# Up weights' second load cut in two, two products of the first step moved, and the last block's sums copied into PSUM before its last splits

## The chip, the core and the metric

The kernel runs on one core of one Trainium2 chip. The metric is the device time of one execution in microseconds. The core has a matrix engine (PE; its weight loads are shown as PEld), three engines for elementwise work (VectorE or DVE, ScalarE or ACT, GpSimd or POOL), SyncE (SP), which here only issues transfers, and 16 DMA engines that all queues share. Engines run side by side; each takes its own instructions in order and waits for the others by semaphores.

## The reference

Four layers on a residual stream of 512 tokens by 1024 features: attention with low-rank keys and values (MLA), an MLP, gated linear attention (GLA), an MLP, and a last RMS norm. All is float32. The change touches the two MLPs, cut to what matters:

```python
def sq_relu_mlp(xn, w_up, w_down):          # w_up 1024 x 4096, w_down 4096 x 1024
    hid = jnp.square(jax.nn.relu(xn @ w_up))
    return hid @ w_down

for i in range(DEPTH):                      # DEPTH = 2
    ...
    x = x + sq_relu_mlp(rms_norm(x, norm_mlp[i]), mlp_w_up[i], mlp_w_down[i])
return rms_norm(x, final_norm)
```

## The kernel before, in words

Every float32 operand of a matmul is split into a rounded high part and a rest (`split`: the high part by ACT, line 110, the rest by DVE, line 113), and each product is three matmuls: high by high, high by low, low by high. A weight tile is split into buffers named `wh` and `wl`, four of each, so that a split can run up to four products ahead of PE.

`mlp` works through the 4096 hidden columns in 8 blocks of 512 (`FB`, `NB`). In the first 7 blocks two multiplications with the weights are each done in 7 products instead of 8, by Strassen's scheme in Winograd's form: sums of quadrants of the weights and of the activations are multiplied, and the results added up in SBUF tiles `S11`, `S12`, `SU`, `S21`, `S5` (the first four lie in the memory of `xT`, and the profile names them so). A step of the loop makes 7 up products for the next block (24 matmuls of 128x256 each, line 958) and 7 down products for the present one (12 matmuls of 128x512 each, line 967). `step_in_halves` (steps 1 to 6) does all the up products and then all the down products. `step` (step 0 of each MLP) mixes them, in an order written as a tuple of functions: `up_t2`, `down_11` and so on. The up products are called "11", T1, T2, "21", T3, "22" and T4 here. In a step with halves they stand in the order 11, T1, T2, 21, T3, 22, T4.

The weights of a step come as named tiles. `fetch(b, name)` loads them for step `b`:

- `A1` and `A2`: 256 columns of the up weights each, 1 MB, in tiles `wraw` of which there are two. `A2`'s first half (`s3`, used by T3) must also have the block "A11" added to it; POOL does so with an accumulating transfer (line 937), which is a software transfer from its own queue. Its second half (`a22`) is used by T4.
- `S1`, `dS1`, `dS3`: 512 KB plain, to which POOL's queue accumulates another 512 KB (line 947). `d11`, `d12`, `d22`: 512 KB plain. All lie in `comb` tiles, one buffer for each name.

A tile is loaded for step `b + 1` when step `b` has split it for the last time: after each product the program calls `after(name)`, which calls `fetch(b + 1, name)`. SP issues the plain transfers in the order of these calls and waits in turn for each buffer to come free, so a load behind a waiting one waits too; POOL does the same with the accumulations, each of which waits until its plain part has landed. In the last step `after` calls `before_next` (first MLP) or `at_the_end` (second MLP), which load what follows.

Two more rules set the order. Instructions are put in order by a scheduler when the program is built, so ACT and DVE hold the splits of later products among the copies and squares of earlier ones. And in a step with halves, "11" goes into the PSUM bank `z`; ACT copies it to `y` (`copied`, line 1090) before T2 may add to `z`.

After the loop the second MLP makes the last block in the plain way, together with the last norm: the sums `S12` and `S11` are copied into PSUM banks (`two_banks("e")` and `("d")`, line 1258), products of the hidden tiles (split by `parts_of_quad`) are added to them there (`row`, line 1272), in the order of token tiles 2, 3, 0, 1, and then the same is done for the other half of the columns.

```python
            for product in (up_t2, down_11, up_t1, down_22, up_22, down_12, up_t3, down_5, down_21, up_t4):
                product()
        ...
            up_product(z, a11, "11", True)
            copied(y, z)
```

Of the kernel before, what the change touches and what calls it, by code (L numbers as in the profile page):

```python
# [18 lines left out]
P = 128  # L19
# [3 lines left out]
ND = D // P  # L23
# [27 lines left out]
def trunk_kernel(ctx: ExitStack, tc: tile.TileContext, t_in: dict, out: bass.AP):  # L51
# [27 lines left out]
    def two_banks(tag):  # L79
        return psum["pool"].tile([P, 1024], F32, tag=f"ps_{tag}", bufs=1, name=uname("ps2"))  # L80
# [302 lines left out]
    def col_chunk(w2d, c0, n):  # L383
        return load(w2d[:, c0 : c0 + n].rearrange("(k p) n -> p k n", p=P), w2d.shape[0] // P, n)
# [430 lines left out]
    def mlp(layer, nrm, nxt=None):  # L815
# [106 lines left out]
        def up_quadrant(b, c, h):  # L922
            cs = slice((b + 1) * FB + c * 256, (b + 1) * FB + c * 256 + 256)
            return w_up[h * KH * P : (h + 1) * KH * P, cs].rearrange("(k p) n -> p k n", p=P)
# [7 lines left out]
        def fetch(b, name):  # L932
            if name in ("A1", "A2"):
                c = int(name[1]) - 1
                W[name] = col_chunk(w_up, (b + 1) * FB + c * 256, 256)
                if c:
                    POOL.dma_start(W[name][:, :KH], up_quadrant(b, 0, 0), accum_op=ALU.add)
                return None
            q = up_quadrant if name == "S1" else down_quadrant
            W[name] = t = by_k(comb(home[name]), KH if name == "S1" else 2)  # L940
            plain, more = {
                "d11": ((0, 0), None), "d12": ((0, 1), None), "d22": ((1, 1), None),
                "S1": ((1, 1), (1, 0)), "dS1": ((1, 1), (1, 0)), "dS3": ((1, 0), (0, 0)),
            }[name]
            first_part = SP.dma_start(t, q(b, *plain))
            if more:
                POOL.dma_start(t, q(b, *more), accum_op=ALU.add)
            return first_part
# [21 lines left out]
        def step(b, q, r, after):  # L970
            opening = nxt is not None
            (q11, q12), (q21, q22) = q

            def begun(src):
                t = two_banks("e")
                ACT.activation(t, src, AF.Copy)
                return t

            def add(total, t):
                if opening:  # L980
                    ACT.activation(total, t, AF.Copy)
                else:
                    DVE.tensor_tensor(total, t, total, ALU.add)

            def onto(tag, total, a, parts, fresh=False):
                t = two_banks(tag)
                if not fresh:
                    ACT.activation(t, total, AF.Copy)
                down_product(t, a, parts, fresh)
                ACT.activation(total, t, AF.Copy)  # L990

            A1, A2, s1 = W["A1"], W["A2"], W["S1"]
            a11, a12, s3, a22 = A1[:, :KH], A1[:, KH:], A2[:, :KH], A2[:, KH:]
            d11, d12, ds1, ds3, d22 = (W[n] for n in ("d11", "d12", "dS1", "dS3", "d22"))

            z = bank("u")
            up_product(z, a11, "11", True)
            y = bank("u")
            ACT.activation(y, z, AF.Copy)

            d = two_banks("d")
            down_product(d, d11, parts_of_quad(q11), True)
            if opening:
                ACT.activation(S11, d, AF.Copy)
            e = two_banks("e") if opening else begun(d)

            up_product(y, a12, "21", False)
            finish(y, 0, 0, r)
            DVE.tensor_tensor(a11, s1, a11, ALU.add)

            down_product(e, d12, parts_of_quad(q21), opening)
            DVE.tensor_tensor(S11, e, S11, ALU.add)
            DVE.tensor_tensor(d11, ds1, d11, ALU.add)
            DVE.tensor_tensor(q12, q22, q12, ALU.subtract)
            DVE.tensor_tensor(q11, q11, q12, ALU.add)

            part = {"e": e}

            def down_11():
                down_product(d, d11, parts_of_quad(q11, -1.0), False)  # L1020
                part["e"] = begun(d)
                DVE.tensor_tensor(d12, d11, d12, ALU.add)
                after("d11")

            def up_t2():
                up_product(z, a11, "T2", False)
                u = part["u"] = tmp()
                ACT.activation(u, z, AF.Copy)
                DVE.tensor_tensor(a12, a11, a12, ALU.add)

            def up_t1():
                w = part["w"] = bank("u")
                up_product(w, s1, "T1", True)
                w2 = part["w2"] = bank("u")
                ACT.activation(w2, w, AF.Copy)
                after("S1")

            def down_22():
                e = part["e"]
                down_product(e, d12, parts_of_quad(q22), False)  # L1040
                add(S12, e)
                after("d12")

            def down_12():
                down_product(d, ds3, parts_of_quad(q12), False)
                add(SU, d)
                after("dS3")
                DVE.tensor_tensor(q22, q22, q11, ALU.subtract)

            def up_22():  # L1050
                w = part["w"]
                up_product(w, a12, "22", False)
                c = tmp()
                DVE.tensor_tensor(c, w, part["u"], ALU.add)
                finish(c, 0, 1, r)
                after("A1")

            def up_t3():
                up_product(z, s3, "T3", False)
                v = tmp()  # L1060
                ACT.activation(v, z, AF.Copy)
                c = tmp()
                DVE.tensor_tensor(c, part["w2"], v, ALU.add)
                finish(c, 1, 1, r)

            def down_5():
                onto("e", S5, ds1, parts_of_quad(q22, -1.0), True)
                after("dS1")
                DVE.tensor_tensor(q21, q21, q11, ALU.subtract)

            def down_21():
                onto("d", S21, d22, parts_of_quad(q21, -1.0), opening)
                after("d22")

            def up_t4():
                up_product(z, a22, "T4", False)
                finish(z, 1, 0, r)
                after("A2")

            for product in (up_t2, down_11, up_t1, down_22, up_22, down_12, up_t3, down_5, down_21, up_t4):  # L1080
                product()

        def step_in_halves(b, q, r, after):
# [93 lines left out]
        def before_next(name):  # L1177
            if name in ("d11", "S1", "d12", "dS3"):
                t = by_k(comb(home[name]), 2)
                SP.dma_start(t, x_kept[:, 2 * len(kept) : 2 * len(kept) + 2])  # L1180
                kept.append(t)
            if name in ("A1", "A2"):
                last_raw.append(load(down_cols(len(last_raw)), 4, 512))
            if name == "d12":
                DVE.tensor_tensor(S12, S12, S5, ALU.add)

        def at_the_end(name):
            if name in ("d11", "S1", "d12", "dS3"):
                i = len(last_raw)
                t = by_k(comb(home[name]), 2)  # L1190
                k0 = (NB - 1) * FB + i % 2 * 256
                SP.dma_start(t, w_dn[k0 : k0 + 256, i // 2 * 512 : (i // 2 + 1) * 512].rearrange("(k p) n -> p k n", p=P))
                last_raw.append(t)
            if name == "d12":
                DVE.tensor_tensor(S12, S12, S5, ALU.add)
            if name == "dS1":
                t = comb(home[name])
                SP.dma_start(t, t_in["fin_row"].to_broadcast([P, D]))
                gain.append(t)
                rounded(0)  # L1200
# [12 lines left out]
        if nxt:  # L1213
# [27 lines left out]
            es.close()  # L1241
            return
        hid = {}
        for h, th in ((0, 0), (0, 1), (1, 1), (1, 0)):
            hid[h, th] = parts_of_quad(q[h][th])
        DVE.tensor_tensor(S21, S21, SU, ALU.add)
# [6 lines left out]
        for c in range(2):  # L1253
            for th in (1, 0):
                total = (S11, S12, S21, SU)[2 * c + th]
                if c == 0:
                    o = two_banks("de"[th])
                    ACT.activation(o, total, AF.Copy)
                for i in range(2):
                    cs = slice(i * 512, (i + 1) * 512)  # L1260
                    if c:
                        o = bank("u")
                        ACT.activation(o, total[:, cs], AF.Copy, scale=-1.0)
                    rows[2 * th + i, c] = total[:, cs], o if c else o[:, cs]
# [586 lines left out]
```

## Time and profile before

| what | value |
|---|---|
| time, median of 3 runs | 1063.76 us (1063.44 to 1065.33) |
| time of the profiled execution | 1063.61 us |
| span of the profiled execution | 1061.8 us |
| mean granted clock of PE | 0.993 |
| PE busy | 1040.0 us, 98% |
| DVE busy | 877.6 us, 83% |
| ACT busy | 697.2 us, 66% |
| moved by DMA | 149.97 MB, 141 GB/s on the mean |

The span goes from the first to the last instruction; the 1.8 us between it and the execution's time lie around it. A busy share says how much of the span an engine had an instruction in work, and not that it worked at its best; what an engine waited for is told by the list of waits, and which waits set the end by the chain of work that ended last. The granted clock is the share of its full speed at which PE was let run. In lists of instructions a row has its start in microseconds, its duration, engine, line, operation, what it writes and reads, and in brackets the time that the engine had been idle and what ended it.

### The profile page before, as it was taken

How to read it: one execution, taken by the hardware profiler on the slowest of the kernel's cores; microseconds unless marked ns; L12 is line 12 of the kernel's file. 1: busy time of each engine (PE TensorE's matmuls, PEld its weight loads, DVE VectorE, ACT ScalarE, POOL GpSimd, SP SyncE). 2: the span in 40 equal slices, each digit the busy share in tenths (PEclk: the TensorE clock that was granted, in tenths of full speed). 3: DMA queues.
4: the chain of work that ended last, by engine and by line, in shares of the span. 5: the costliest groups of instructions: out<-in, count | busy, mean ns of one | idle time of the engine just before them, and what ended most of it. 6: DMA issues, size and time to landing. Idle time of an engine off the chain costs nothing.

```text
span 1061.8 us, 15754 instructions
## 1 busy us (share of the span) xinstructions
PE 1040.0 (98%) x5966; PEld 908.1 (86%) x5966; DVE 877.6 (83%) x1340; ACT 697.2 (66%) x1122; POOL 113.9 (11%) x128
## 2 busy tenths in 40 slices
PE   9999999997999999999999999999998999999997
PEld 7788888897899899898888888888897889989976
DVE  7889977976998989988686498469786989998993
ACT  7667754574776776775445565655674777777774
POOL 8410011210011101100000000000011101111000
PEclk9999999998999999999999999999998999999999
DMA  7401244867788688734212312265396777777422
GB/s 230 119 21 40 80 109 129 238 177 163 201 194 204 176 199 203 172 129 130 77 53 85 100 54 80 72 163 147 92 225 161 173 199 197 186 203 190 119 80 80
DMA packets 120493, 149.97 MB, mean 141 GB/s; under 512 B 9344, under 2 KB 86144, under 8 KB 120288
## 3 DMA queue, kind: packets, MB, share of 16 engines
q1 hardware_dynamic: 95920, 117.76, 34.5%
q0 software_dynamic: 22400, 29.36, 17.6%
q10 hardware_dynamic: 2096, 1.84, 0.5%
q8 instruction: 47, 0.77, 0.3%
q14 instruction: 30, 0.25, 0.1%
HBM read 144.49 MB, written 4.19 MB: 140 GB/s over the span
## 4 chain that ended last, share of the span: by engine, by line
PE 89%; ACT 4%; DVE 3%; DMA 3%; issue 1%; SPq 0%; ACTq 0%; DVEq 0%; POOLq 0%
PE ps L967 25%; PE ps L958 23%; PE ps L118 10%; PE ps L120 10%; PE ps L119 10%; DMA wraw<-in_mlp_w_up_dram 2%; PE ps L1237 2%; PE ps L1492 1%; PE ps L135 1%; PE ps L1272 1%; DVE wl L113 1%; ACT wh L110 1%; PE ps L421 1%; PE ps L1619 1%; DMA xT<-in_x_dram 0%
## 5 line engine op out<-in xcount | busy, mean ns | idle before, releaser
L967 PE MATMUL ps<-wh,set 128*128 128x512 f32 x784 | 245.8, 390 | 0.3 <-ACT set L110 0.3
L110 ACT ACTIVATE wh<-wraw 128x1024 fp32r<-128x1024 f32 x139 | 146.4, 1056 | 123.9 <-PE ps L119 41.6
L113 DVE TENSOR_TENSOR wl<-wraw,wh 128x1024 fp32r<-128x1024 f32 x139 | 169.6, 1220 | 54.6 <-ACT wh L110 54.3
L967 PEld LDWEIGHTS ps<-wh,set 128*128 128x128 f32 x784 | 147.0, 188 | 30.8 <-ACT set L110 0.7
L958 PE MATMUL ps<-T,wh 128*128 128x256 f32 x896 | 159.5, 280 | 11.3 <-ACT ps L1090 11.3
L113 DVE TENSOR_TENSOR wl<-comb,wh 128x1024 fp32r<-128x1024 f32 x112 | 136.7, 1221 | 19.5 <-ACT wh L110 19.5
L967 PE MATMUL ps<-wl,set 128*128 128x512 f32 x392 | 152.6, 389 | 0.0
L958 PEld LDWEIGHTS ps<-T,wh 128*128 128x128 f32 x896 | 139.0, 192 | 12.3 <-ACT ps L1090 11.7
L110 ACT ACTIVATE wh<-comb 128x1024 fp32r<-128x1024 f32 x112 | 118.3, 1056 | 45.1 <-issue 26.6
L958 PE MATMUL ps<-T,wl 128*128 128x256 f32 x448 | 125.4, 280 | 0.0
L958 PE MATMUL ps<-set,wh 128*128 128x256 f32 x672 | 117.3, 276 | 0.0
L118 PE MATMUL ps<-set,wh 128*128 128x512 f32 x280 | 109.7, 392 | 0.0
L119 PE MATMUL ps<-set,wh 128*128 128x512 f32 x280 | 109.7, 392 | 0.0
L120 PE MATMUL ps<-set,wl 128*128 128x512 f32 x280 | 109.4, 391 | 0.0
L958 PEld LDWEIGHTS ps<-set,wh 128*128 128x128 f32 x672 | 102.7, 188 | 1.2
L958 PE MATMUL ps<-set,wl 128*128 128x256 f32 x336 | 92.7, 276 | 0.0
L958 PEld LDWEIGHTS ps<-T,wl 128*128 128x128 f32 x448 | 86.1, 192 | 0.1
L967 PEld LDWEIGHTS ps<-wl,set 128*128 128x128 f32 x392 | 73.6, 188 | 14.6
L958 PEld LDWEIGHTS ps<-set,wl 128*128 128x128 f32 x336 | 63.2, 188 | 0.0
L110 ACT ACTIVATE set<-set 128x512 fp32r<-128x512 f32 (+1 forms) x70 | 42.3, 604 | 30.7 <-PE ps L967 29.1
L120 PEld LDWEIGHTS ps<-set,wl 128*128 128x128 f32 x280 | 52.6, 188 | 11.1
L119 PEld LDWEIGHTS ps<-set,wh 128*128 128x128 f32 x280 | 52.6, 188 | 11.0 <-DVE set L750 0.2
(414 smaller groups left out, 2023.5 us busy)
## 6 DMA issues: line engine op xcount, KB each, us to landing
comb<-in_mlp_w_down_dram SPq DMA_DIRECT2D x74, 512.0 KB, 3.6
wraw<-in_mlp_w_up_dram SPq DMA_DIRECT2D x32, 1024.0 KB, 5.6
comb<-in_mlp_w_down_dram POOLq DMA_DIRECT2D x28, 512.0 KB, 6.0
wraw<-in_gla_w_in_dram SPq DMA_DIRECT2D x12, 1024.0 KB, 5.2
comb<-in_mlp_w_up_dram SPq DMA_DIRECT2D x14, 512.0 KB, 3.6
comb<-in_mlp_w_up_dram POOLq DMA_DIRECT2D x14, 512.0 KB, 6.5
wraw<-in_mlp_w_up_dram POOLq DMA_DIRECT2D x14, 512.0 KB, 6.1
wraw<-in_mla_w_o_dram SPq DMA_DIRECT2D x4, 1024.0 KB, 5.0
```

The source lines that it names most:

```text
L110: order(ACT.activation(hi, src, AF.Copy))
L113: lo_eng.tensor_tensor(lo, src, f(hi), ALU.subtract)
L118: PE.matmul(psum, wh, xh, start=start, stop=False)
L119: PE.matmul(psum, wh, xl, start=False, stop=False)
L120: PE.matmul(psum, wl, xh, start=False, stop=stop)
L135: PE.transpose(psum, src, ident[: src.shape[0], : src.shape[0]])
L421: PE.matmul(p, w[:, i, j * P : (j + 1) * P], x, start=start, stop=stop)
L958: PE.matmul(o, a_, x_, start=start and j == 0 and k == 0 and n == 0, stop=k == KH - 1 and n == 2, skip_group_check=True)
L967: PE.matmul(o, x_, w_, start=start and k == 0 and n == 0, stop=k == 1 and n == 2, skip_group_check=True)
L1237: PE.matmul(p, a, x, start=False, stop=k == 3 and n == 2, skip_group_check=True)
L1272: PE.matmul(o, a, b_, start=False, stop=k == 3 and n == 2, skip_group_check=True)
L1492: PE.matmul(p[:, t - t0], k[:, t * P : (t + 1) * P], moving[:, t], start=True, stop=True)
```

## The change

Three things are changed.

1. `fetch` loads `A2` in two transfers of 512 KB instead of one of 1 MB, the first half first; POOL's accumulation onto the first half stands between them and waits for the first half alone. This goes for all 14 loads of `A2` (7 in each MLP).
2. In `step`, `up_t3` moves ahead of `down_12` and `up_t4` ahead of `down_5` and `down_21`. With `up_t4` goes `after("A2")`, the load of `A2` for step 1.
3. In the last step `S12` gets `S5` added after `dS1` (when `S5` is complete) instead of after `d12`; and in the last block the copy of `S12` into PSUM is called ahead of the last `parts_of_quad`.

```diff
             if name in ("A1", "A2"):
                 c = int(name[1]) - 1
-                W[name] = col_chunk(w_up, (b + 1) * FB + c * 256, 256)
-                if c:
-                    POOL.dma_start(W[name][:, :KH], up_quadrant(b, 0, 0), accum_op=ALU.add)
+                if c == 0:
+                    W[name] = col_chunk(w_up, (b + 1) * FB, 256)
+                    return None
+                W[name] = t = sb.tile([P, ND, 256], F32, tag="wraw", bufs=2, name=uname("wraw"))
+                SP.dma_start(t[:, :KH], up_quadrant(b, 1, 0))
+                POOL.dma_start(t[:, :KH], up_quadrant(b, 0, 0), accum_op=ALU.add)
+                SP.dma_start(t[:, KH:], up_quadrant(b, 1, 1))
                 return None
...
-            for product in (up_t2, down_11, up_t1, down_22, up_22, down_12, up_t3, down_5, down_21, up_t4):
+            for product in (up_t2, down_11, up_t1, down_22, up_22, up_t3, down_12, up_t4, down_5, down_21):
...
-            if name == "d12":
+            if name == "dS1":
                 DVE.tensor_tensor(S12, S12, S5, ALU.add)
...
-            if name == "d12":
+            if name == "dS1":
                 DVE.tensor_tensor(S12, S12, S5, ALU.add)
-            if name == "dS1":
                 t = comb(home[name])
                 SP.dma_start(t, t_in["fin_row"].to_broadcast([P, D]))
...
         hid = {}
+        loaded = {1: two_banks("e")}
+        ACT.activation(loaded[1], S12, AF.Copy)
         for h, th in ((0, 0), (0, 1), (1, 1), (1, 0)):
             hid[h, th] = parts_of_quad(q[h][th])
...
                 if c == 0:
-                    o = two_banks("de"[th])
-                    ACT.activation(o, total, AF.Copy)
+                    if th not in loaded:
+                        loaded[th] = two_banks("d")
+                        ACT.activation(loaded[th], total, AF.Copy)
+                    o = loaded[th]
```

SP's queue in step 0 of the first MLP, before. The rows are the loads for step 1: `A1`, `dS3`, `dS1`, `d22`, `A2`, and then `S1` and `A1` for step 2.

```order
L140 DMA wraw_2610<-in_mlp_w_up_dram 128x8x256
L945 DMA comb_2631<-in_mlp_w_down_dram 128x2x512
L945 DMA comb_2690<-in_mlp_w_down_dram 128x2x512
L945 DMA comb_2714<-in_mlp_w_down_dram 128x2x512
L140 DMA wraw_2747<-in_mlp_w_up_dram 128x8x256
L945 DMA comb_2813<-in_mlp_w_up_dram 128x4x256
L140 DMA wraw_2946<-in_mlp_w_up_dram 128x8x256
```

The same place after (lines are 4 later, and L939 and L941 are the halves of `A2`):

```order
L140 DMA wraw_2611<-in_mlp_w_up_dram 128x8x256
L949 DMA comb_2667<-in_mlp_w_down_dram 128x2x512
L939 DMA wraw_2702<-in_mlp_w_up_dram 128x4x256
L941 DMA wraw_2702<-in_mlp_w_up_dram 128x4x256
L949 DMA comb_2726<-in_mlp_w_down_dram 128x2x512
L949 DMA comb_2750<-in_mlp_w_down_dram 128x2x512
L949 DMA comb_2815<-in_mlp_w_up_dram 128x4x256
L140 DMA wraw_2948<-in_mlp_w_up_dram 128x8x256
```

`A2` has moved past `dS1` and `d22`. On POOL's queue its accumulation has moved past that of `dS1` in the same way.

ACT's queue at the same place, before, from the copy of `d` into `e` (L976) on. `wraw_2357` is `A2` of step 0, whose last split, for T4, is `wh_2716`; L1061 is the copy of T3's result out of `z`.

```order
L976 ACTIVATE ps_529_2517<-ps_515_2393 128x1024
L110 ACTIVATE wh_2614<-comb_2354 128x1024
L110 ACTIVATE wh_2635<-wraw_2357 128x1024
L1035 ACTIVATE ps_2551<-ps_2522 128x512
L110 ACTIVATE set_2155<-set_2145 128x512
L981 ACTIVATE xT<-ps_529_2517 128x1024
L110 ACTIVATE wh_2673<-comb_2344 128x1024
L110 ACTIVATE wh_2697<-comb_2360 128x1024
L981 ACTIVATE xT<-ps_515_2393 128x1024
L860 ACTIVATE set_2146<-tmp_2607 128x512
L110 ACTIVATE wh_2716<-wraw_2357 128x1024
```

After (L980, L1039, L985 and L1065 are the old L976, L1035, L981 and L1061; `wh_2671` is now the split for T4):

```order
L980 ACTIVATE ps_529_2518<-ps_515_2394 128x1024
L110 ACTIVATE wh_2613<-wraw_2357 128x1024
L110 ACTIVATE wh_2650<-comb_2354 128x1024
L1039 ACTIVATE ps_2552<-ps_2523 128x512
L110 ACTIVATE set_2155<-set_2145 128x512
L985 ACTIVATE xT<-ps_529_2518 128x1024
L110 ACTIVATE wh_2671<-wraw_2357 128x1024
L110 ACTIVATE wh_2709<-comb_2344 128x1024
L110 ACTIVATE wh_2733<-comb_2361 128x1024
L860 ACTIVATE set_2146<-tmp_2608 128x512
L1065 ACTIVATE tmp_2641<-ps_2363 128x512
```

The split for T4 stands where the first down product behind `down_12` had its split, four rows higher.

The end of the second MLP on DVE, before. L1149 adds the last product of `S12`, L1195 adds `S5` to it, L1250 scales the last gain.

```order
L1250 TENSOR_SCALAR comb_10249<-comb_10249 128x1024
L113 TENSOR_TENSOR set_7291<-set_7283,set_7290 128x512
L1149 TENSOR_TENSOR xT<-ps_1691_10217,xT 128x1024
L113 TENSOR_TENSOR set_7289<-set_7281,set_7288 128x512
L1195 TENSOR_TENSOR xT<-xT,sum_7292 128x1024
L1152 TENSOR_TENSOR xT<-ps_1679_10131,xT 128x1024
```

After (L1199 adds `S5`, L1255 scales the gain, L1153 adds the last product):

```order
L1199 TENSOR_TENSOR xT<-xT,sum_7299 128x1024
L113 TENSOR_TENSOR set_7298<-set_7290,set_7297 128x512
L1255 TENSOR_SCALAR comb_10264<-comb_10264 128x1024
L1153 TENSOR_TENSOR xT<-ps_1691_10231,xT 128x1024
L113 TENSOR_TENSOR set_7296<-set_7288,set_7295 128x512
L113 TENSOR_TENSOR set<-comb_10312,set 128x512
L1156 TENSOR_TENSOR xT<-ps_1679_10145,xT 128x1024
```

The addition of `S5` has moved ahead of the gain and of the last product, so `S12` is complete at L1153 and not one addition of 128x1024 later. On ACT the copy of `S12` into PSUM has changed places with the split of the last hidden tile, which stood just ahead of it.

## The prediction, made before the changed kernel had run

> **What bounds the kernel now.** I read the page first, then PE's waits, then the chain of work that ended last, then stretches of the span by busy time and clock, and last the single rows around the two places that these name. The page and PE's waits (who waited for whom; us in total, times, longest):
>
> ```profile
> PE 1040.0 (98%) x5966; PEld 908.1 (86%) x5966; DVE 877.6 (83%) x1340; ACT 697.2 (66%) x1122; POOL 113.9 (11%) x128
> PE ps L958 <- ACT ps L1090: 11.3, 2, 6.1
> PE ps L1272 <- ACT ps L1258: 1.4, 1, 1.4
> ```
>
> PE is the bound nearly everywhere. It stands still for others at three places worth a change: twice in an up product (6.1 us, and so 5.2 us the other time), once 1.4 us in the last block. The chain (start, us, what) shows the two: the first MLP, and below the dots the second, then the last block.
>
> ```profile
> 236.37 0.96 ACT wh L110
> 237.36 1.24 DVE wl L113
> 238.61 10.63 DMA wraw<-in_mlp_w_up_dram
> 249.31 0.56 issue
> 249.87 5.84 DMA wraw<-in_mlp_w_up_dram
> 255.78 1.06 ACT wh L110
> 256.84 0.49 ACT ps L1090
> 257.38 15.85 PE ps L958 x120
> 273.22 19.07 PE ps L967 x84
> 292.30 19.09 PE ps L958 x168
> ...
> 805.33 16.61 PE ps L958 x120
> ...
> 1031.62 0.63 ACT set L110
> ```
>
> To be read so: `A2` for step 1 can only be loaded when step 0's T4 has been split (237.36). 1 MB lands 10.6 us later, POOL adds the second block, which takes until 255.71, ACT splits `s3` for T3, and only behind that split comes ACT's copy of `z` into `y` (L1090), for which PE needs to begin T2. So PE does not lack T3's weights yet; it stands because ACT's queue does. The gap also costs after its end: five products (x120) take 15.85 us, while seven undisturbed ones (x168) take 19.09, so five should take 13.64. The stretches say why (columns: us, PE, PEld, DVE, ACT, POOL busy, granted clock, DMA share, GB/s):
>
> ```profile
> 258.00:260.00 2.00, 2.00 (x11) 2.00 (x11) 1.30 (x3) 1.27 (x3) 0.00 (x0) 0.50 0.00 0
> 300.00:480.00 180.00, 180.00 (x1181) 163.96 (x1180) 162.97 (x180) 135.45 (x190) 19.66 (x17) 1.00 0.71 183
> ```
>
> After the gap PE ran at half clock for a while; without gaps it holds 1.00 for 180 us.
>
> **The products of step 0 and the split load of A2.** What is to be gained: first MLP 6.1 + (15.85 - 13.64 = 2.21) = 8.3 us; second 5.2 + (16.61 - 13.64 = 2.97) = 8.2 us. Together 16.5 us. [...]
>
> Is the gap really covered afterwards? PE stood from 257.38 - 6.1 = 251.3. ACT needs 1.55 us from the start of T3's split (255.78) to the end of the copy (257.33). So the accumulation onto `A2` must have landed by 249.7 for PE to see nothing, and in the second MLP by 800.1 - 1.55 = 798.6. When does it land now? Rows of ACT, DVE and POOL, and how long single transfers took (KB, us from issue to landing: `dS1` plain, issued behind DVE's 231.67 split, then POOL's `dS1` in the first and the second MLP):
>
> ```profile
> 230.58 1.05 ACT L110 ACTIVATE wh<-comb 128x1024 fp32r<-128x1024 f32 x1
> 231.67 1.22 DVE L113 TENSOR_TENSOR wl<-comb,wh 128x1024 fp32r<-128x1024 f32 x1 [1.17 <-ACT wh L110]
> 236.97 1.20 POOL L947 DMA_DIRECT2D comb<-in_mlp_w_down_dram  x1 [1.34 <-DMA comb<-in_mlp_w_down_dram]
> comb<-in_mlp_w_down_dram SPq DMA_DIRECT2D x1, 512.0 KB, 3.4
> comb<-in_mlp_w_down_dram POOLq DMA_DIRECT2D x1, 512.0 KB, 10.0
> ...
> 786.15 1.20 POOL L947 DMA_DIRECT2D comb<-in_mlp_w_down_dram  x1 [1.39 <-DVE wl L113]
> comb<-in_mlp_w_down_dram POOLq DMA_DIRECT2D x1, 512.0 KB, 10.4
> ```
>
> The order of the change puts T4's split in the place of this split of `dS1`: ACT 230.58, DVE 231.67 to 232.89. So SP issues the first half of `A2` at about 232.9 instead of 238.61, and it lands like `dS1`'s plain part did, 3.4 us later, at 236.3. POOL then takes the slot that `dS1` had (236.97) and the accumulation should land like that one, 10.0 us later: 247.0, that is 2.7 us ahead of need. The second MLP by the same steps: 786.15 + 10.4 = 796.6, 2.0 us ahead of 798.6. The bounds are the short accumulation of the chain (5.84: 242.8) and, for the worst, the old way from issue to landing, 255.71 - 238.61 = 17.1 us counted from 232.9: 250.0, which would leave a stall of 0.3 us. I take 10.0, since it is the row of the same queue at the same moment, with no more traffic beside it: 1 MB of `A2` then, `A2`'s second half and a later `dS1` now. So both gaps go whole.
>
> What the moves cost. T3 comes one product earlier; its split and that of `down_12` change places, which delays the load of `dS3` by one split (1.22 us), with nothing that needs it before step 1's last products. T4 now follows T3 with one product between, and may not write `z` before ACT has copied T3's result (the old L1061). T3's end releases one split of weights on ACT, then a square (L860), then that copy. By their rows, here from the old place:
>
> ```profile
> 236.27 1.06 ACT L110 ACTIVATE wh<-wraw 128x1024 fp32r<-128x1024 f32 x1
> 242.22 0.62 ACT L860 ACTIVATE set<-tmp 128x512 f32<-128x512 f32 x1
> 238.49 0.58 ACT L1061 ACTIVATE tmp<-ps 128x512 f32<-128x512 f32 x1
> ```
>
> 1.06 + 0.62 + 0.58 = 2.26 us, against 19.09 / 7 = 2.73 us of the product that covers them: 0.5 us to spare; if the square's input came late, each microsecond over that would be paid in full, once per MLP. I take 0. `dS1` and `d22` go behind `A2` on SP: their own buffers come free only after 232.9, so SP does not hold them; `dS1`'s accumulation goes behind that of `A2` (a rival below). The 12 later loads of `A2` have one more issue each on SP, which waits for buffers most of the time; PE has no wait there now, so 0. The split itself has a price on the DMA engines; the median transfers of the profile's page (KB, us to landing):
>
> ```profile
> comb<-in_mlp_w_down_dram SPq DMA_DIRECT2D x74, 512.0 KB, 3.6
> wraw<-in_mlp_w_up_dram SPq DMA_DIRECT2D x32, 1024.0 KB, 5.6
> ```
>
> Two halves one after the other would be 2 x 3.6 = 7.2 against 5.6 us, so 1.6 us more at most, still inside the 2.7 and 2.0; I take 0. [...]
>
> **The last block.** Rows of DVE, then ACT, then PE:
>
> ```profile
> 1027.81 0.69 DVE L1250 TENSOR_SCALAR comb<-comb 128x1024 f32<-128x1024 f32 x1
> 1028.41 0.69 DVE L113 TENSOR_TENSOR set<-set,set 128x512 fp32r<-128x512 f32 x1
> 1029.13 1.23 DVE L1149 TENSOR_TENSOR xT<-ps,xT 128x1024 f32<-128x1024 f32 x1
> 1030.87 1.22 DVE L1195 TENSOR_TENSOR xT<-xT,sum 128x1024 f32<-128x1024 f32 x1
> 1032.00 1.22 DVE L1152 TENSOR_TENSOR xT<-ps,xT 128x1024 f32<-128x1024 f32 x1
> 1032.15 2.13 ACT L1258 ACTIVATE ps<-xT 128x1024 f32<-128x1024 f32 x2
> 1033.22 22.31 PE L1272 MATMUL ps<-set,set 128*128 128x512 f32 x96 [1.41 <-ACT ps L1258]
> ```
>
> `S12` was complete at 1032.09 (L1195), and ACT's copy of 1.07 us let PE go on at 1033.22. The split ahead of the copy on ACT (start 1031.62, end 1032.25 in the chain above) came free at the same moment, so either move alone would give next to nothing, and both are made. Now DVE does the same four operations from 1027.81 in another order; a 1.22 us operation lets the next start after 1.13 (1030.87 to 1032.00), a 0.69 us one after 0.60. So L1195's addition starts at 1027.81, the split at 1028.94, the gain at 1029.54, the last product's addition at 1030.14, which ends at 1031.37. The copy then ends near 1032.50 and PE goes on 0.7 us earlier. Bounds: 0 (DVE gets there late) and 1.4 (no wait left). After that 96 matmuls, 22.31 us, and the same tail.
>
> **The sum.** On the profiled execution's own time, 1063.61 (span 1061.8 and 1.8 around it; 0.15 under the median, which I leave out): 1063.61 - 8.3 - 8.2 - 0.7 = 1046.4 us.
>
> **Rivals.** *The accumulation still lands late.* It would have to take over 12.7 us in the first MLP or 12.4 in the second; 10.0 and 10.4 have been seen on a busy machine, and `A2`'s own 10.63 for 1 MB shows how crowded these microseconds are. Landing 3 us after need in both: 3 us each, 1052.4; with the clock lost again (2.2 and 3.0), 1057.6. Chance 0.14, mostly with small remainders.
>
> *The wait moves to `dS1`, and the kernel is slower.* `dS1`'s accumulation now starts behind `A2`'s. In step 1 DVE adds `dS1` to `d11` in its queue ahead of the split of the second down product:
>
> ```profile
> 267.33 1.23 DVE L1131 TENSOR_TENSOR comb<-comb,comb 128x1024 f32<-128x1024 f32 x1
> ```
>
> Without the gap that comes at 259.0. The second down product would begin at 273.22 - 8.3 + 2.7 = 267.6, less 2.5 us for the addition and the split: from a landing after 265 on PE stands. To eat up the gain it would have to stand some 6 us in each MLP, with about 2.6 us more for the clock: from a landing after 271 the kernel is slower. Landing at 274 would mean 9 + 2.6 us each, 23.2 in all, less the 17.2 gained: 1069.6. Against it: the plain part lands by about 240, and then 34 us would be needed where 10.0 were. Chance 0.05.
>
> *It doesn't do what it says*: the accumulation waits for both halves or ACT finds another wait at the same place, and PE stands as before: 1063.6. For it speaks only that the copy hangs on whatever ACT has ahead of it. Chance 0.03.
>
> **How the numbers follow.** Forecast 0.78. All gaps gone whole would be 1063.61 - 8.3 - 8.2 - 1.4 = 1045.7; the low end is a little below, 1045.2, and the high end 1051.0 takes in the smaller remainders of the first rival (2.3 us each). A measurement of this kernel can tell about 0.2%, 2.1 us, from no change. Faster 0.78 + 0.14 = 0.92, same 0.03, slower 0.05.
>
> **What would show it.** Right: PE's waits lose the L1090 row; the chain goes through PE alone from T4 to the down products of step 1; the clock stays 1.00 there and its mean rises; seven products of step 1 take 19.1 us in both MLPs; about 0.7 us remain before L1279, the old L1272. The split of `A2` has helped if POOL's `A2` is issued near 237 and lands by 249. Wrong: a wait of PE for ACT or DVE inside step 0 (T4 behind the copy of T3), or a DVE wait for a transfer at the new L1135.

## The result and the profile after

The changed kernel takes 1046.17 us (median of 4 runs, 1045.81 to 1046.67) against 1064.12 us: ratio 0.983, 95% interval 0.9813 to 0.9847. The profiled execution took 1046.67 us, with a span of 1044.9. Forecast were 1046.4 us, range 1045.2 to 1051.0. PE's busy time and the wait that is left, from the page and from PE's waits (who waited for whom; us in total, times, longest):

```profile
PE 1035.0 (99%) x5966; PEld 903.9 (87%) x5966; DVE 876.9 (84%) x1340; ACT 696.8 (67%) x1122; POOL 114.3 (11%) x128
PE ps L1279 <- ACT ps L1248: 1.1, 1, 1.1
```

The row of 11.3 us on ACT's copy of `z` (old L1090, now L1094) is gone from the waits. The chain of work that ended last (start, us, what) runs through PE alone where it used to go through DVE, a transfer and ACT; the rows around the dots are from the first MLP, the second, and the last block:

```profile
234.87 2.75 PE ps L971 x12
237.62 2.77 PE ps L962 x24
240.39 5.47 PE ps L971 x24
245.86 19.09 PE ps L962 x168
284.02 19.09 PE ps L962 x168
...
786.07 19.09 PE ps L962 x168
...
824.23 19.09 PE ps L962 x168
...
1016.14 22.34 PE ps L1279 x96
```

Seven up products of step 1 take 19.09 us in both MLPs, as undisturbed ones do. The stretches of step 0 and step 1 (us; busy time of PE, PEld, DVE, ACT, POOL; granted clock, DMA share, GB/s) show PE busy without a hole and the clock at 1.00:

```profile
228.00:290.00 62.00, 62.00 (x421) 56.98 (x420) 54.25 (x60) 45.65 (x62) 9.98 (x8) 1.00 0.88 216
770.00:830.00 60.00, 60.00 (x409) 55.23 (x408) 54.70 (x61) 44.03 (x60) 9.97 (x8) 1.00 0.88 216
```

Where the time came from, by start times in the two traces: the second step's seven products in the first MLP begin at 284.02 instead of 292.30, 8.3 us sooner; the same in the second MLP at 824.23 instead of 841.01, 16.8 us sooner; the last block's products at 1016.14 instead of 1033.22, 17.1 us sooner. The second MLP itself began 8.55 us sooner (743.39 instead of 751.94, PE's first group of 16 at line 910). So the first gap gave 8.3 us, the stretch between the MLPs 0.3, the second gap 8.2, and the last block 0.3.

The steps of the transfer, as POOL's and ACT's rows show them, with the time from issue to landing of POOL's addition on `A2` in the first and the second MLP (KB, us):

```profile
237.66 1.31 POOL L940 DMA_DIRECT2D wraw<-in_mlp_w_up_dram  x1 [1.50 <-DVE wl L113]
wraw<-in_mlp_w_up_dram POOLq DMA_DIRECT2D x1, 512.0 KB, 10.2
248.59 1.06 ACT L110 ACTIVATE wh<-wraw 128x1024 fp32r<-128x1024 f32 x1
249.54 0.59 ACT L1094 ACTIVATE ps<-ps 128x512 f32<-128x512 f32 x1
...
777.95 1.31 POOL L940 DMA_DIRECT2D wraw<-in_mlp_w_up_dram  x1 [1.87 <-DVE wl L113]
wraw<-in_mlp_w_up_dram POOLq DMA_DIRECT2D x1, 512.0 KB, 9.4
```

The first half of `A2` was issued at 233.03 and took 3.9 us. The addition lands at 247.86 (237.66 + 10.2), and ACT comes to the split of `s3` at 248.59 without having waited for it.

### The profile page after: what moved, and what is told of

The parts are those of the page before. It is cut to its first block, busy times and chain, and to the rows that moved or that the text cites. A ratio compares the mean times of both kernels' runs of the same rounds, so it can differ in the third digit from the quotient of the medians.

```text
span 1044.9 us, 15747 instructions
## 1 busy us (share of the span) xinstructions
PE 1035.0 (99%) x5966; PEld 903.9 (87%) x5966; DVE 876.9 (84%) x1340; ACT 696.8 (67%) x1122; POOL 114.3 (11%) x128
## 3 DMA queue, kind: packets, MB, share of 16 engines
q1 hardware_dynamic: 96144, 117.76, 35.4%
q0 software_dynamic: 22400, 29.36, 18.0%
## 4 chain that ended last, share of the span: by engine, by line
PE 94%; DVE 3%; ACT 2%; issue 0%; DMA 0%; ACTq 0%; SPq 0%; DVEq 0%
PE ps L971 25%; PE ps L962 25%; PE ps L118 10%; PE ps L120 10%; PE ps L119 10%; PE ps L1279 2%; PE ps L1240 2%; PE ps L1499 1%; PE ps L135 1%; PE ps L421 1%; PE ps L1626 1%; DVE wl L113 1%; PE ps L1766 0%; PE ps L1549 0%; PE ps L684 0%
## 5 line engine op out<-in xcount | busy, mean ns | idle before, releaser
L962 PE MATMUL ps<-T,wh 128*128 128x256 f32 x896 | 154.9, 275 | 0.0
L962 PEld LDWEIGHTS ps<-T,wh 128*128 128x128 f32 x896 | 135.4, 188 | 0.4
L962 PEld LDWEIGHTS ps<-set,wh 128*128 128x128 f32 x672 | 102.6, 188 | 1.3
L119 PEld LDWEIGHTS ps<-set,wh 128*128 128x128 f32 x280 | 52.6, 188 | 11.1 <-DVE set L750 0.2
L118 PEld LDWEIGHTS ps<-set,wh 128*128 128x128 f32 x280 | 52.6, 188 | 10.7
```

Of the source, the lines that this page charges most:

```text
L118: PE.matmul(psum, wh, xh, start=start, stop=False)
L119: PE.matmul(psum, wh, xl, start=False, stop=False)
L962: PE.matmul(o, a_, x_, start=start and j == 0 and k == 0 and n == 0, stop=k == KH - 1 and n == 2, skip_group_check=True)
```

## The experiments

Each edit is to the kernel named. Each ratio is to runs of the kernel before that were made beside it; their medians lay between 1063.44 and 1064.41 us. Code is cut to the lines that matter.

**Which part does the work.** The split of the load alone (the new `fetch`, everything else as before):

```diff
...
+                SP.dma_start(t[:, :KH], up_quadrant(b, 1, 0))
+                POOL.dma_start(t[:, :KH], up_quadrant(b, 0, 0), accum_op=ALU.add)
+                SP.dma_start(t[:, KH:], up_quadrant(b, 1, 1))
```

> The kernel before with one edit: A2 is loaded in two halves (and POOL's addition waits for the first half only); products and last block as before. Theory (the landing of the addition on A2 sets PE's gap): the first half is issued at 238.6 and lands about 3.9 us later, POOL issues the addition near 243.1, and it takes between 5.8 us (as before, little else on the way) and 10.2 us (as in the changed kernel): landing at 249 to 253.3 against a need at 249.7, so PE stands 0 to 3.6 us in the first MLP instead of 6.1; second MLP: issue 786.1, first half 5.5 us, addition from 792, 5.9 to 9.4 us, landing 798 to 801.4 against 798.6, so 0 to 2.8 us instead of 5.2. [...] Time 1047.5 to 1055, middle 1051. Rival A (the product order does all the work, the split is only in its way): PE still stands 5 us or more in both MLPs, 1060 to 1064. Rival B (the split by itself is enough): no wait left, 1047.

Measured: 1060.8 us, ratio 0.9966 (0.9953 to 0.9979). PE's wait, the chain, and the median landing time of the two halves:

```profile
PE ps L962 <- ACT ps L1094: 9.6, 2, 5.3
248.54 6.03 DMA wraw<-in_mlp_w_up_dram
256.26 15.81 PE ps L962 x120
wraw<-in_mlp_w_up_dram SPq DMA_DIRECT2D x2, 512.0 KB, 10.1
```

The gaps stay at 5.3 and 4.3 us, and the time lies outside the 1047.5 to 1055 that was expected and in the range of rival A (5 us or more in both MLPs, which came out as 5.3 and 4.3). The expected range has 1.1 us at most for the clock behind gaps of up to 3.6 and 2.8 us (1055 less 1047.5 and 6.4); that was the author's estimate, and no run shows it: further down, gaps of 2.1 and 1.8 us cost no clock, and one of 3.6 us did. One number failed: the first half was to land 3.9 us after its issue, and it took 9.6 (the second 10.6), about as long as the whole 1 MB before (10.6).

What held it was on its way beside it. In the kernel before, `dS1`'s plain part, issued ahead of `A2`, had landed at 236.3, before `A2` was issued at 238.61, and `d22` landed at about 239.8. But POOL's additions on `dS3` (234.43, 8.3 us) and on `dS1` (236.97, 10.0 us) ran until 242.7 and 247.0. Two stretches of the kernel before (the last two columns are the DMA engines' busy share and GB/s) show the engines fully busy in both, at half the rate in the first, with both additions on their way, of that in the second, where the last of them ends:

```profile
240.00:242.00 2.00, 2.00 (x11) 1.65 (x10) 2.00 (x3) 1.65 (x2) 0.00 (x0) 1.00 1.07 188
246.00:248.00 2.00, 2.00 (x20) 2.00 (x19) 2.00 (x4) 1.87 (x3) 0.00 (x0) 1.00 1.09 369
```

So where the text below calls `A2` behind `dS1`, that means behind the addition on it above all. No run holds back the addition alone; its share is argued from these rows. Now the product order alone:

```diff
-            for product in (up_t2, down_11, up_t1, down_22, up_22, down_12, up_t3, down_5, down_21, up_t4):
+            for product in (up_t2, down_11, up_t1, down_22, up_22, up_t3, down_12, up_t4, down_5, down_21):
```

> The kernel before with one edit: T3 and T4 each one or two products sooner, as in the change; A2 still one load of 1 MB, last block as before. Theory (landing sets the gap): A2 is issued near 232.9 and takes 10.6 us, POOL adds from about 244, 5.8 to 10.2 us: landing 249.9 to 254.2 against 249.7, so PE stands 0.2 to 4.5 us in the first MLP; second MLP in the old times: issue about 782.6, 11.0 us, addition from 794.2, 5.9 to 9.4 us, landing 800.1 to 803.6 against 798.6, so 1.5 to 5.0 us. Time 1049 to 1060, middle 1053. Rival (the split does nothing that the order does not do): no wait left, 1047.

Measured: 1046.64 us, 0.9833 (0.9818 to 0.9848), nearly the whole gain. The waits; then the load of `A2` as one piece, and POOL's addition:

```profile
PE ps L958 <- ACT ps L1090: 0.2, 1, 0.2
PE ps L1272 <- ACT ps L1258: 1.4, 1, 1.4
wraw<-in_mlp_w_up_dram SPq DMA_DIRECT2D x1, 1024.0 KB, 6.4
239.84 1.31 POOL L937 DMA_DIRECT2D wraw<-in_mlp_w_up_dram  x1 [3.34 <-DVE set L1132]
wraw<-in_mlp_w_up_dram POOLq DMA_DIRECT2D x1, 512.0 KB, 8.6
```

The rival was right: issued ahead of `dS1`, `d22` and the addition on `dS1`, 1 MB lands in 6.4 us, the addition on it at 248.4, and 0.2 us of the gaps is left. The changed kernel with `A2` loaded whole again says the same from the other side:

> The changed kernel with A2 loaded whole again, so product order and last block alone. Theory (the product order alone brings the load 5.7 us forward and to the head of the line, and 1 MB then takes 6.4 us instead of 10.6): the same time as the changed kernel within 0.3 us, PE's wait at the copy of z at most 0.2 us. Rival (the prediction's picture, where A2 whole would take 10.6 us as before): gaps of 2 to 4 us in both MLPs, 1050 or more.

Measured: 1045.93 us (0.9831, 0.9817 to 0.9844), with 1045.92 for the changed kernel in the same runs. The split is worth nothing that these runs can tell; it brings the landing from 248.25 (issue 239.15, 9.1 us) to 247.86, and neither is late.

**Sooner, or first in line?** The product order does two things to `A2`: its buffer comes free 5.7 us sooner, and it goes ahead of `dS1`, `d22` and the addition on `dS1`. The second alone, on the kernel before (the loads of `dS1`, `d22` and the addition on `dS1` held behind those of `A2`, all else in its old order):

```diff
...
+                if b == 0 and name in ("dS1", "d22"):
+                    held.append(name)
+                    return
                 fetch(b + 1, name)
+                if b == 0 and name == "A2":
+                    for n in held:
+                        fetch(b + 1, n, True)
```

> The kernel before with its products, splits and last block in their old order; only the loads dS1 and d22 of step 1 (and POOL's addition on dS1) are issued behind those of A2 instead of ahead of them. T4's split still frees A2's buffer near 238.4. Theory (half of what the product order brings is that A2 goes to the head of the line): 1 MB takes about 6.4 us instead of 10.6, POOL adds from 245.5, 5.8 to 8.6 us: landing 251.3 to 254.1 against a need at 249.7, so PE stands 1.6 to 4.4 us instead of 6.1; second MLP 0.4 to 3.1 us instead of 5.2. Time 1050 to 1060, middle 1056. Rival (only the moment at which the buffer comes free counts): gaps as before, 1063 to 1064.

Measured: 1055.0 us, 0.9909 (0.989 to 0.9927). Its profiled execution was the shortest of four (1051.97 with a mean clock of 0.999, the others 1054.24 to 1055.97 with 0.996 to 0.997), so its rows tell the mechanism, not the median; the others have no profile, and what they lost stays open:

```profile
PE ps L972 <- ACT ps L1104: 3.9, 2, 2.1
wraw<-in_mlp_w_up_dram SPq DMA_DIRECT2D x1, 1024.0 KB, 6.0
245.57 6.43 DMA wraw<-in_mlp_w_up_dram
253.66 13.90 PE ps L972 x120
```

Issued at the old moment (238.89), but first, the load takes 6.0 us; the addition lands at 252.00 instead of 255.71. So of the 7.9 us by which the landing moved in the changed kernel, place in line alone gives 3.7; the other 4.2 came when the moment was earlier too. T4 one product later, so that it is early but behind `dS1` and its addition again (`d22` stays behind `A2`):

```diff
-            for product in (..., up_22, up_t3, down_12, up_t4, down_5, down_21):
+            for product in (..., up_22, up_t3, down_12, down_5, up_t4, down_21):
```

> The changed kernel with T4 one product later, between down_5 and down_21: A2 in two halves, the last block's edit in, but dS1 is in line ahead of A2 again. T4's split comes near 235.6. Theory (place in line and moment both count): a half takes about 7 us behind dS1, POOL adds from 243.2, 9 us: landing about 252, a gap of 2 to 3 us in each MLP, short enough that the clock stays at 1.00: 1050 to 1052 us. Rival A (the moment alone): first half 3.9 us, addition 10.2 us, landing at 250.3, gaps of 0.6 us at most: 1046 to 1047.5. Rival B (any gap halves the clock): 2 us more for each gap, 1054 to 1056.

Measured: 1051.37 us, 0.9877 (0.9862 to 0.9892): the expected time by another sum, one gap of 3.6 us with lost clock in the first MLP and none in the second. That the clock stays at 1.00 in gaps of 2 to 3 us was the author's estimate; the longest gap of the first steps that left it there in these profiles was the 2.1 us of `A2` late but first. PE's wait and the chain of the first MLP; below the dots ACT's rows in the second:

```profile
PE ps L962 <- ACT ps L1094: 3.6, 1, 3.6
241.41 11.82 DMA wraw<-in_mlp_w_up_dram
254.91 15.40 PE ps L962 x120
...
794.44 0.58 ACT L1094 ACTIVATE ps<-ps 128x512 f32<-128x512 f32 x1
798.20 2.01 ACT L110 ACTIVATE wh<-wraw 128x1024 fp32r<-128x1024 f32 x2 [3.17 <-DMA wraw<-in_mlp_w_up_dram]
```

In the second MLP the scheduler put ACT's copy of `z` ahead of the split of `s3`. ACT then stood 3.2 us for the same late transfer, with nothing behind it that PE lacked at once. That is the mechanism of the prediction with its opposite: the gap is not made by missing weights but by what is queued behind the split.

Here the first half took 6.0 us and the second 8.9, so the 1 MB was on its way for 9.3 us (234.72 to 244.0) with `d22` behind it: `d22`'s place was not what made it slow. The addition on `A2`, running beside those on `dS3` and `dS1`, took 11.8. Landing less gap gives the moment at which the weights are needed in the first MLP: 255.71 - 6.1 = 249.6 before, 254.57 - 5.3 = 249.3 with the split alone, 252.00 - 2.1 = 249.9, 253.23 - 3.6 = 249.6. The prediction had 249.7.

**The cover of T4.** T4 directly behind T3, without the product that covers ACT's copy:

```diff
-            for product in (..., up_22, up_t3, down_12, up_t4, down_5, down_21):
+            for product in (..., up_22, up_t3, up_t4, down_12, down_5, down_21):
```

> The changed kernel with T4 directly behind T3 (the product down_12, which stood between them, comes after T4). Theory (T4 may not write z until ACT has copied T3's result, and 2.73 us of the product between covers that): in the changed kernel T3 ends at 234.87 and the copy at 236.85, so PE now stands 2.0 us in each MLP ahead of T4, 4.0 in all, clock still 1.00 since the gaps are short: 1050.2 us. Rival A (the queue on ACT lets the copy through at once, 0.6 us): two gaps of 0.7 us, 1047.6. Rival B (any gap halves the clock for some microseconds): 2 more us for each, about 1054.

Measured: 1046.51 us, 0.9829 (0.9812 to 0.9845), no wait at T4. All three expectations fell, since the edit did not do on PE what it says in the code: the scheduler put ten matmuls of the down product between T3 and T4 by itself. That the clock stays at 1.00 in gaps of 2.0 us was not tried here; with `A2` late but first it stayed there in gaps of 2.1 and 1.8 us.

```profile
235.20 2.30 PE ps L971 x10
237.50 2.75 PE ps L962 x24
240.25 5.93 PE ps L971 x26
PE ps L1279 <- ACT ps L1248: 0.4, 1, 0.4
```

`A2` came earlier still (POOL's addition at 235.94), and that brought nothing more.

**The last block.** Its edit alone on the kernel before:

```diff
-            if name == "d12":
+            if name == "dS1":
                 DVE.tensor_tensor(S12, S12, S5, ALU.add)
...
+        loaded = {1: two_banks("e")}
+        ACT.activation(loaded[1], S12, AF.Copy)
```

> The kernel before with only the last block's edit: sum of S12 and S5 sooner, copy into PSUM ahead of the splits. Both gaps of the first steps stay (11.3 us). Theory: as in the changed kernel, PE's wait ahead of the last block's products falls from 1.4 to about 1.1 us: 1063.3 us, not to be told from the kernel before. Rival (the prediction's own term of 0.7 us, and the changed kernel only had bad luck with a transfer): the wait is 0.7 us.

Measured: 1062.78 us, 0.9988 (0.9979 to 0.9998), and a wait of 0.2 us, less than either expectation. The cause is a late transfer. One row each of the changed kernel, of T4 at once and of this kernel, the split of a piece of the last down weights that stands on ACT's queue ahead of the copies of `S5`:

```profile
1009.19 0.63 ACT L110 ACTIVATE set<-comb 128x512 fp32r<-128x512 f32 x1 [0.96 <-DMA comb<-in_mlp_w_down_dram]
```

```profile
1009.30 0.64 ACT L110 ACTIVATE set<-comb 128x512 fp32r<-128x512 f32 x1 [0.26 <-DMA comb<-in_mlp_w_down_dram]
```

```profile
1024.75 0.63 ACT L110 ACTIVATE set<-comb 128x512 fp32r<-128x512 f32 x1
PE ps L1275 <- ACT ps L1244: 0.2, 1, 0.2
```

ACT waits 0.96, 0.26 and 0 us for that transfer, and PE then waits 1.1, 0.4 and 0.2: the transfer's lateness plus 0.2. (With `A2` whole they are 0.65 and 0.8.) The sum hangs on this split twice: `S5` is copied behind it on ACT, and DVE makes the rests of the same pieces just ahead of the sum. In the changed kernel `S5` was complete at 1011.31, and DVE came from the second rest to the sum at 1011.47:

```profile
1011.47 1.22 DVE L1199 TENSOR_TENSOR xT<-xT,sum 128x1024 f32<-128x1024 f32 x1
```

The weights themselves are for the second half of the columns, some 11 us into the last block's products. The changed kernel once more:

> The changed kernel once more, on the same chip as the next three, to compare with. The runs so far say that PE's wait ahead of the last block is 0.2 us plus the time that ACT stands for a transfer of the last block's down weights (0.96 us in the changed kernel's profile, 0.26 with T4 at once, none with the last block's edit alone: waits of 1.1, 0.4 and 0.2). So this wait should come out between 0.2 and 1.2 us, and the median between 1045.3 and 1046.3 us.

Measured: 1045.92 us (0.9834, 0.9821 to 0.9847); its profiled execution, 1045.57, has a wait of 0.2 us, where that of the first profile, 1046.67, has 1.1. The copy alone, with the sum in its old place:

```diff
-            if name == "dS1":
+            if name == "d12":
                 DVE.tensor_tensor(S12, S12, S5, ALU.add)
```

> The changed kernel with DVE's sum S12 + S5 back in its old place; only the copy into PSUM is written ahead of the last splits. Theory of the prediction (either move alone gives next to nothing): on ACT the copy then still stands behind the last split, as before, and the wait is 1.4 us: 0.3 to 1.2 us slower than the changed kernel, 1046.5 to 1047.5. Rival (the copy is what counted): the wait falls to 1.1 us or less.

Measured: 1048.88 us, 0.9856 (0.984 to 0.9873), with this row:

```profile
PE ps L1280 <- ACT ps L1249: 1.6, 1, 1.6
```

So the copy's place in the code does nothing. On ACT it still stands behind the last split, as in the kernel before; and with the sum alone moved, all five queues come out, but for buffer numbers, instruction for instruction as in the changed kernel. The edit of the last block is the sum. That this kernel is some 2.3 to 3.0 us slower than the changed one, where the wait explains 0.5 to 1.4, stays open: its profiled execution, 1047.57, was the shortest of four, and the others (1048.79 to 1048.99) have no profile.

**Towards a better version.** The late splits (`rounded(1)`) were held behind ACT's copy of `S12`:

```diff
-        ACT.activation(loaded[1], S12, AF.Copy)
+        put = ACT.activation(loaded[1], S12, AF.Copy)
...
-        rounded(1)
+        with tc.issue_after(put.ins):
+            rounded(1)
```

> The changed kernel with the splits of the last block's second half of the down weights issued behind ACT's copy of S12 into PSUM. Theory (what is left of the wait hangs on ACT, which splits a late transfer ahead of its copies of S5, which DVE needs for S12 + S5): no wait of PE for the copy is left, 0.2 to 1.1 us less than the changed kernel beside it: about 1045.2 us; the late splits are needed 11 us later, so they cost nothing. Rival (DVE's own queue is the limit, transfer or not): a wait of 0.4 us or more stays.

Measured: 1046.55 us, 0.9838 (0.9825 to 0.9852), no better than the 1045.92 beside it. The wait for the first copy went, and another came: five splits, 2.64 us, ahead of the second copy.

```profile
1014.81 2.64 ACT set L110 x5
PE ps L1280 <- ACT ps L1265: 0.5, 1, 0.5
```

With `A2` whole as well:

> Both edits: A2 whole, and the late splits behind the copy. If the split of A2 is worth nothing, the same time as with the late splits alone, about 1045.2 us; if the split is worth its 0.6 us of earlier landing, up to 0.5 us more.

Measured: 1046.29 us, 0.9838 (0.9825 to 0.9852), the same. With the splits held behind both copies (`put` set at the second one):

> The changed kernel with the late splits issued behind ACT's copies of both sums into PSUM, S12 and S11. The first try put them between the two copies: the wait for the first copy went, but PE then stood 0.5 us for the second, behind five splits of 2.64 us together. Theory: now neither copy waits for a split; the products of the last block start when the down products end and run on: 0.2 to 1.1 us less than the changed kernel, about 1045.3 us. Rival (the splits are then late for the second half's products, or the order of the last operations gets worse): 1046 to 1047.

Measured: 1046.13 us, 0.9826 (0.981 to 0.9843). No wait of PE is left in the last block, and yet nothing is gained. Against the changed kernel's second profile PE is done at the same time (1037.37 there, 1037.36 here), and after it come 6.4 us there and 7.0 here, since ACT now scales an earlier row (0.71 us, L1300) ahead of the last row's chain. No version beat the changed kernel by more than these runs can tell.

## Why the prediction was right, point by point

*The gaps and their clock cost.* Forecast 8.3 and 8.2 us; by start times the first gave 8.3 and the second 8.2. The chain from T4's split over `A2` to the copy of `z` was the right one, and its deadline (249.7) holds in four kernels within 0.4 us.

*When `A2` lands.* Forecast 247.0; measured 247.86, since the first half took 3.9 us and not 3.4, so that POOL issued at 237.66, not 236.97, and the addition took 10.2, not 10.0. So 1.8 us to spare, not 2.7. The outcome was right, and the old 10.63 us for 1 MB did show "how crowded these microseconds are". What the prediction missed is that, by the rows behind the first experiment, the crowd is mostly the additions on `dS3` and `dS1`, and that the order alone takes the load out of it: 1 MB took 5.6 us (`A2` whole) and 6.4 us (order alone) when issued near 232.9, and 6.0 us at the old moment when `dS1`, `d22` and the addition were held behind it. The split, which the forecast let carry the transfer through, was not needed.

*The cover of T4.* Forecast 0.5 us to spare. In the profile T3's copy starts at 236.27 and takes 0.58, and T4 starts at 237.62 (the chain above): 0.8. The danger was not put to the test: when T4 was written directly behind T3, the scheduler filled the place between them.

```profile
236.27 0.58 ACT L1065 ACTIVATE tmp<-ps 128x512 f32<-128x512 f32 x1
259.11 1.22 DVE L1135 TENSOR_TENSOR comb<-comb,comb 128x1024 f32<-128x1024 f32 x1
```

*The rival of `dS1`.* Its addition was issued at 242.97 and landed at 251.0; DVE took it at 259.11 without a wait, 14 us before the 265 from which PE would have stood. The other rivals did not come about; the late landing came in the experiments with a gap of 3.6 us.

*The last block.* Forecast 0.7 us, measured 0.3 in the first profile and 1.2 where no transfer was late. The order of DVE's operations was right; what did not hold is the fixed time in "So L1195's addition starts at 1027.81". DVE came there from the two splits that hang on the late transfer, for which ACT stood 0.52 us in the profile before. In the changed kernel it stood 0.96, 0.44 more, and the sum began 0.44 later than by the forecast (1011.47; 1027.81 less the 16.78 us won by then is 1011.03). With T4 between, ACT stood 0.52 again, and PE's wait was the 0.7 us of the prediction. The rows are of the kernel before and of T4 between:

```profile
1025.53 0.63 ACT L110 ACTIVATE set<-comb 128x512 fp32r<-128x512 f32 x1 [0.52 <-DMA comb<-in_mlp_w_down_dram]
```

```profile
1014.47 0.64 ACT L110 ACTIVATE set<-comb 128x512 fp32r<-128x512 f32 x1 [0.52 <-DMA comb<-in_mlp_w_down_dram]
```

So this term can't be forecast to better than the transfer's lateness, 0 to 0.96 us in these profiles. And "either move alone would give next to nothing" held for the copy alone only: the sum alone is the whole edit.

*The sum.* 17.2 us forecast; 1063.61 - 1046.67 = 16.9 between the profiled executions, and 17.5 and 17.95 between medians. The gaps gave the 16.5 of the forecast; the last block gave 0.4 less than its term in that execution; 0.3 came between the MLPs, for which the sum has no term; and what follows the start of the last block's products took 0.2 longer (28.76 us of the span instead of 28.58). That the total came out within 0.3 us is in part luck, since the last block alone varies by more.

## What to carry to other kernels

When a transfer is late, look at what is on its way beside it before its size, accumulating transfers above all (a byte of theirs took about twice the DMA engines' time of a plain one in the kernel before): the same 1 MB took 5.6 to 6.4 us ahead of `dS1`, `d22` and the addition, and 10.6 behind them, and cutting it in two there bought 1.1 us of the 7.9. Here a reorder that frees the buffer sooner and puts the load first made the split needless; test the parts alone before keeping both. And where a sum is to come sooner, look at what stands ahead of it on every engine that it needs: splits that hang on a transfer, and whose own data are needed much later, can hold it.

## What the hardware showed that was not expected

The shorter gap lost more by the clock. Stretches of 0.1 us (granted clock third from the end) of the kernel before, first and second MLP, hold the moments of the change between 1.00 and 0.50:

```profile
254.70:254.80 0.10, 0.00 (x0) 0.00 (x0) 0.00 (x0) 0.00 (x0) 0.00 (x0) 0.59 1.16 184
261.50:261.60 0.10, 0.10 (x3) 0.10 (x3) 0.10 (x1) 0.00 (x0) 0.00 (x0) 0.77 0.00 0
804.20:804.30 0.10, 0.00 (x0) 0.00 (x0) 0.00 (x0) 0.10 (x1) 0.00 (x0) 0.82 1.21 195
811.00:811.10 0.10, 0.10 (x3) 0.10 (x2) 0.00 (x0) 0.10 (x1) 0.00 (x0) 0.54 0.21 20
```

A mean of 0.59 between 1.00 and 0.50 puts the change 18% into the slice, at 254.72; the others come to 261.55, 804.26 and 811.09. Both slow stretches last 6.83 us, but PE was back at 257.38 in the first and at 805.33 in the second. So it ran at half clock for 4.17 us after the gap of 6.1 us and for 5.76 us after that of 5.2, and lost half of that, 2.1 and 2.9 (2.2 and 3.0 by the products). With the split alone, in the second MLP, it was 3.1 us (803.41 to 806.51) after a gap of 4.3. The gaps of 2.1 and 1.8 us in the profile with `A2` late but first cost no clock (1.00 in every slice of 0.1 us around them), the one of 3.6 us with T4 between did (five products took 15.40 us instead of 13.64). From what length on a gap costs clock, and what sets the moment at which the clock comes back, no run shows.

POOL's addition on `A2` for step 1 of the first MLP (512 KB) took 5.8 to 11.8 us in the profiles that were read for it, shortest where no other was on its way on POOL's queue when it was issued (5.8 in the kernel before, 6.0 with the split alone, 6.4 with `A2` late but first) and longest with two others still on their way (11.8 with T4 between). Over the whole kernel before, POOL's queue moved 29.36 MB in 17.6% of the DMA engines' time and the plain queue 117.76 MB in 34.5%, so a byte that is accumulated took about twice the engines' time of a plain one, which fits the two rates above (188 and 369 GB/s).
